# Two-layer hybrid decoder trunk on one core: fixed order at the end of the first gate/up blocks, second block's low parts last, first scale on VectorE

## Chip, cores and metric

The kernel runs on 1 core of one Trainium2 chip. The time is the device time of one execution in microseconds (us); lower is better. The kernel before took 1039.81 us, the median of 3 runs (1039.14 to 1040.87).

## What is computed

Two layers; each is a half-step SwiGLU, a mixer of sixteen attention heads (eight of one kind, eight of another), and a second half-step SwiGLU. A final RMS norm follows. Input x is 256 x 1024 float32, the inner width is 2816.

```python
def rms_norm(x, g):
    xf = x.astype(jnp.float32)
    y = xf * lax.rsqrt(jnp.mean(xf * xf, axis=-1, keepdims=True) + EPS)
    return (y * g.astype(jnp.float32)).astype(x.dtype)

def swiglu(x, w_gate, w_up, w_down):
    return (jax.nn.silu(x @ w_gate) * (x @ w_up)) @ w_down
...
    for l in range(DEPTH):
        x = x + 0.5 * swiglu(rms_norm(x, norm_ffn1[l]), w_ffn1_gate[l], w_ffn1_up[l], w_ffn1_down[l])
        x = x + hybrid_mixer(rms_norm(x, norm_mix[l]), w_in[l], ...)
        x = x + 0.5 * swiglu(rms_norm(x, norm_ffn2[l]), w_ffn2_gate[l], w_ffn2_up[l], w_ffn2_down[l])
    return rms_norm(x, norm_final)
```

## The kernel before

**Weights as a stream.** All weights are cut into 326 blocks of 128 x 1024 float32 (512 KB; a few are smaller), in order of use. `Stream.loads` (L223) issues their DMAs on SyncE into 5 raw buffers (`wraw`). `Stream.split` (L241) makes two tiles of each: ScalarE casts the block to a high part (`whi`, L254), VectorE subtracts it from the raw block for the low part (`wlo`, L283), which frees the raw buffer. There are 7 slots for such pairs of parts; a slot comes free when TensorE has read its block for the last time. A product of full precision is then high times high, high times low and low times high.

**A SwiGLU phase** (`ffn`, L593). The 2816 inner columns are 22 column blocks j of 128. For each j there is a gate block and an up block of weights. `wide` (L555) multiplies one of them: for each of 8 row blocks k one matmul of the high part with 512 columns (x high and x low side by side, L560), and one of the low part with 256 columns (x high, L562). Even j write two PSUM banks with the tag psB, odd j write psC and psD. `read` (L622) takes the banks out: ScalarE copies one half (L626), VectorE adds the other (L627), into a tile `hs`; the banks are free for the next j of the same parity after that. `finish` (L629) multiplies with the row scale on GpSimd (L635, tile `rbc`), takes Silu on ScalarE, multiplies again on GpSimd (L637, `rbc5`) and on VectorE (L639), and splits the result into `hp` high (ScalarE, L640) and low (VectorE, L642). `down` (L653) multiplies that with the down block of weights (L539 to L541) into four psA banks.

**The start.** In the first phase the products of j = 0 are made by `first_pair` (L564) and those of j = 1 by `wide`. The sums of squares of x are made meanwhile (`x_start_squares`, L437, ScalarE and GpSimd). `norm_start` (L500) adds them over partitions with two matmuls (L505), VectorE copies the two columns to `ss` (L507), and `inv_rms` (L472) takes the inverse root by a start value and two steps, 13 small operations on 128 x 2 elements on GpSimd. On VectorE the same function needs 10 operations and leaves out the factor `INV`. `norm_bcast` (L510) spreads the result with two transposing matmuls (L514), after which ScalarE writes `rbc` (L517) and `rbc5` (L521).

**Later phases.** In the other three SwiGLU phases `gu_two` (L614) works on j = 0 and j = 1 together through `two_halves` (L580): the first half of k for all four blocks, while the second half of x is still being transposed, and then the second half.

**What sets the order.** The program is recorded in the order of the Python code, and a scheduler then orders each engine's instructions by its own estimate of when each can start, with the recorded order as priority; at that point it also gives out the slots. `tc.issue_after(i)` holds an instruction behind i. Within one engine the order is then fixed, and an instruction that waits holds up those behind it.

Of the kernel before, what the change touches and what calls it, by code (L numbers as in the profile page):

```python
# [26 lines left out]
OP = mybir.AluOpType  # L27
AX = mybir.AxisListType

D, S, L, DH = 1024, 256, 2, 64  # L30
FF = 2816
KT = D // 128
# [49 lines left out]
def all_units(phases):  # L82
    return [u for ph, l in phases for u in phase_units(ph, l)]
# [227 lines left out]
def trunk(ctx, tc, xin, wst, w1st, gains, glast, cst, small, out, phases=PHASES, n_raw=5, n_hl=7):  # L311
    nc = tc.nc
    V, A, G, T = nc.vector, nc.scalar, nc.gpsimd, nc.tensor
# [7 lines left out]
    st = Stream(nc, wst, all_units(phases), rawp, hlp, n_raw, n_hl)  # L321
# [8 lines left out]
    def bank(tag):  # L330
        return ps.tile([128, 512], F32, name="ps" + tag, tag="ps" + tag, bufs=BUFS[tag])
# [40 lines left out]
    state = {}  # L372
# [97 lines left out]
    INV = -3.0 / 16  # L470

    def inv_rms(ss, eng):  # L472


        n = ss.shape[-1]
        v = base.tile([128, 2, 2], F32, name="nv", bufs=2)[:, :, :n]
        y = base.tile([128, 2], F32, name="ny", bufs=2)[:, :n]
        t = base.tile([128, 2], F32, name="nt", bufs=2)[:, :n]
        u = base.tile([128, 2], F32, name="nu", bufs=2)[:, :n]

        def plus_times(o, a, c, b, scale):
            if eng is V:
                V.scalar_tensor_tensor(o, a, c, b, op0=OP.add, op1=OP.mult)
            else:
                G.tensor_scalar(u, a, c, scale, op0=OP.add, op1=OP.mult)
                G.tensor_mul(o, u, b)

        eng.tensor_scalar(v[:, 0], ss, 1.0 / D, EPS, op0=OP.mult, op1=OP.add)
        eng.tensor_scalar(y.bitcast(I32), v[:, 0].bitcast(I32), -0.5, float(0x5F3759DF), op0=OP.mult, op1=OP.add)
        eng.tensor_scalar(v[:, 1], v[:, 0], 9.0 / 64, None, op0=OP.mult)  # L490
        eng.tensor_mul(t, y, y)
        eng.tensor_mul(t, t, v[:, 0])
        plus_times(t, t, -10.0 / 3, t, 1.0)
        plus_times(y, t, 5.0, y, 1.0)
        eng.tensor_mul(t, y, y)
        eng.tensor_mul(t, t, v[:, 1])
        plus_times(y, t, -3.0, y, INV)
        return y

    def norm_start():  # L500

        b = bank("A")
        sq = state["sq"]
        for blk in range(2):
            T.matmul(b[:, blk:blk + 1], sq[:, 0, blk * 128:(blk + 1) * 128], ones, start=True, stop=True)  # L505
        ss = base.tile([128, 2], F32, name="ss")
        V.tensor_copy(ss, b[:, :2])  # L507
        state["rs"] = inv_rms(ss, G)

    def norm_bcast(half):  # L510

# [19 lines left out]
    def three(o, hi, lo, xh, xl, first, last):  # L531
        T.matmul(o, hi, xh, start=first, stop=False, skip_group_check=True)  # L532
        T.matmul(o, hi, xl, start=False, stop=False, skip_group_check=True)  # L533
        T.matmul(o, lo, xh, start=False, stop=last, skip_group_check=True)  # L534

    def across(o, t, parts, hi, lo, first, last):

# [5 lines left out]
    def blk128(t, k):  # L543
        return t[:, k * 128:(k + 1) * 128]

    def narrow_pair(o, us, ks):

        xh, xl = state["xh"], state["xl"]
        for k in ks:
            for i, u in enumerate(us):  # L550
                hi, lo = u[1]
                three(o[:, i * S:(i + 1) * S], blk128(hi, k), blk128(lo, k), xh[:, k], xl[:, k], k == i == 0,
                      k == KT - 1)

    def wide(o, u, ks):  # L555

        hi, lo = u[1]
        for k in ks:
            x = state["x2"][:, k]
            T.matmul(o, blk128(hi, k), x.rearrange("p a t -> p (a t)"), start=k == 0, stop=k == KT - 1,  # L560
                     skip_group_check=True)
            T.matmul(o[:, S:], blk128(lo, k), x[:, 0], start=False, stop=k == KT - 1, skip_group_check=True)  # L562

    def first_pair(os, us):  # L564

# [14 lines left out]
    def two_halves(work):  # L580


        for n, (f, us) in enumerate(work):
            f(range(KT // 2))
            if n == 0:
                state.pop("late")()
        for f, us in work:
            f(range(KT // 2, KT))
            for u in us:
                st.done(u[0])  # L590


    def ffn(pi, name, l):  # L593
# [5 lines left out]
        def gu_open(j):  # L599
            b = pend[j] = [bank(t) for t in gu_tags[j % 2]]  # L600
            return b, [st.use(what, name, l, j) for what in ("gate", "up")]

        def gu(j, mid=None):
            b, us = gu_open(j)
            if j == 0 and pi == 0:
                first_pair(b, us)
                return
            for o, u in zip(b, us):
                wide(o, u, range(KT))
                st.done(u[0])  # L610
                if mid:
                    mid = mid()
# [38 lines left out]
        last = nxt == len(phases)  # L651
# [95 lines left out]
    def mixer(pi, l):  # L747
# [4 lines left out]
        def feature_one(o, u, first):  # L752
            hi, lo = u[1]
            for k in range(KT):
                three(o, blk128(hi, k), blk128(lo, k), xh[:, k], xl[:, k], first and k == 0, k == KT - 1)
            st.done(u[0])
# [577 lines left out]
```

## Time and profile before

| what | value |
|---|---|
| median of 3 runs | 1039.81 us |
| the profiled execution | 1037.38 us |
| its span, first to last instruction | 1035.6 us |
| TensorE busy | 1000.6 us (97% of the span) |
| VectorE busy | 688.5 us (66%) |
| ScalarE busy | 593.3 us (57%) |
| GpSimd busy | 326.1 us (31%) |
| chain that ended last, TensorE's share | 83% |
| mean granted TensorE clock | 0.999 |

The profiled execution is one run; it took 2.43 us less than the median of the three timed runs. In a row of the timeline the first number is the start in us from the beginning of the span, the second the us until the end of the row's last instruction; what stands in brackets is how long the engine was idle before the row and what ended that. Matmuls are pipelined: the next one starts before the row's end, so that distances are read from start to start. The trace writes x for the tile `x2`, and leaves numbers of tiles out.

### The profile page before, as it was taken

How to read it: one execution, taken by the hardware profiler on the slowest of the kernel's cores; microseconds unless marked ns; L12 is line 12 of the kernel's file. 1: busy time of each engine (PE TensorE's matmuls, PEld its weight loads, DVE VectorE, ACT ScalarE, POOL GpSimd, SP SyncE). 2: the span in 40 equal slices, each digit the busy share in tenths (PEclk: the TensorE clock that was granted, in tenths of full speed). 3: DMA queues.
4: the chain of work that ended last, by engine and by line, in shares of the span. 5: the costliest groups of instructions: out<-in, count | busy, mean ns of one | idle time of the engine just before them, and what ended most of it. 6: DMA issues, size and time to landing. Idle time of an engine off the chain costs nothing.

```text
span 1035.6 us, 16186 instructions
## 1 busy us (share of the span) xinstructions
PE 1000.6 (97%) x5861; PEld 861.0 (83%) x5861; DVE 688.5 (66%) x1187; ACT 593.3 (57%) x1137; POOL 326.1 (31%) x425
## 2 busy tenths in 40 slices
PE   9999999998998999999999999999999989999997
PEld 7788888898776888888888888889888778888885
DVE  6766666589865766566676666566986648666664
ACT  6745555457766655555565555545677747555552
POOL 3622232145641422222232223121475313222230
PEclk9999999999999999999999999999999999999999
DMA  8685776455444466666556677764543426666531
GB/s 268 241 279 186 274 240 218 145 171 157 114 126 125 154 198 196 188 197 186 163 182 203 186 234 239 262 196 138 181 131 108 143 82 208 194 209 193 193 122 41
DMA packets 52848, 188.21 MB, mean 182 GB/s; under 512 B 6368, under 2 KB 6496, under 8 KB 51616
## 3 DMA queue, kind: packets, MB, share of 16 engines
q1 hardware_dynamic: 49680, 182.04, 55.4%
q10 hardware_dynamic: 3088, 5.14, 2.0%
q8 instruction: 46, 0.75, 0.3%
q14 instruction: 34, 0.28, 0.1%
HBM read 182.04 MB, written 1.05 MB: 177 GB/s over the span
## 4 chain that ended last, share of the span: by engine, by line
PE 83%; DVE 7%; ACT 5%; issue 2%; DMA 2%; POOL 1%; ACTq 0%; POOLq 0%; DVEq 0%
PE psB L560 15%; PE psA L539 9%; PE psA L540 9%; PE psA L541 9%; PE psB L562 8%; PE psD L560 8%; PE psC L560 7%; PE psD L562 4%; PE psC L562 4%; DVE wlo L283 3%; PE psA L533 2%; PE psA L532 2%; PE psA L534 2%; ACT whi L254 1%; PE psA L398 1%
## 5 line engine op out<-in xcount | busy, mean ns | idle before, releaser
L283 DVE TENSOR_TENSOR wlo<-wraw,whi 128x1024 fp32r<-128x1024 f32 x325 | 408.2, 1259 | 242.1 <-ACT whi L254 240.5
L254 ACT CAST whi<-wraw 128x1024 fp32r<-128x1024 f32 (+1 forms) x326 | 339.5, 1044 | 304.2 <-issue 175.4
L560 PE MATMUL psB<-x,whi 128*128 128x512 f32 x688 | 243.1, 394 | 3.4 <-DVE hs L627 3.3
L635 POOL TENSOR_TENSOR hs<-hs,rbc 128x256 f32<-128x256 f32 x88 | 75.0, 853 | 380.3 <-DVE hs L627 364.6
L562 PE MATMUL psB<-x,wlo 128*128 128x256 f32 x688 | 192.5, 280 | 0.0
L560 PEld LDWEIGHTS psB<-x,whi 128*128 128x128 f32 x688 | 129.2, 188 | 32.5 <-DVE hs L627 4.3
L541 PE MATMUL psA<-wlo,hp 128*128 128x512 f32 x352 | 136.9, 389 | 0.0
L540 PE MATMUL psA<-whi,hp 128*128 128x512 f32 x352 | 136.8, 389 | 0.0
L539 PE MATMUL psA<-whi,hp 128*128 128x512 f32 x352 | 136.2, 390 | 0.0
L562 PEld LDWEIGHTS psB<-x,wlo 128*128 128x128 f32 x688 | 129.4, 188 | 1.4
L637 POOL TENSOR_TENSOR hs<-hs,rbc 128x256 f32<-128x256 f32 x88 | 102.9, 1170 | 80.5 <-ACT hs L636 80.5
L560 PE MATMUL psC<-x,whi 128*128 128x512 f32 x352 | 124.9, 392 | 0.0
L560 PE MATMUL psD<-x,whi 128*128 128x512 f32 x352 | 124.8, 392 | 0.0
L562 PE MATMUL psC<-x,wlo 128*128 128x256 f32 x352 | 98.6, 280 | 0.9 <-DVE wlo L283 0.9
L562 PE MATMUL psD<-x,wlo 128*128 128x256 f32 x352 | 98.4, 280 | 0.0
L560 PEld LDWEIGHTS psC<-x,whi 128*128 128x128 f32 x352 | 66.1, 188 | 14.5
L560 PEld LDWEIGHTS psD<-x,whi 128*128 128x128 f32 x352 | 66.1, 188 | 14.4
L541 PEld LDWEIGHTS psA<-wlo,hp 128*128 128x128 f32 x352 | 66.1, 188 | 13.9
L539 PEld LDWEIGHTS psA<-whi,hp 128*128 128x128 f32 x352 | 66.0, 188 | 13.7
L540 PEld LDWEIGHTS psA<-whi,hp 128*128 128x128 f32 x352 | 66.1, 188 | 12.3
L532 PE MATMUL psA<-x,whi 128*128 128x256 f32 x256 | 72.8, 284 | 1.2 <-ACT PT L1010 0.8
L533 PE MATMUL psA<-x,whi 128*128 128x256 f32 x256 | 72.3, 283 | 0.7 <-DVE x L380 0.7
(229 smaller groups left out, 1586.3 us busy)
## 6 DMA issues: line engine op xcount, KB each, us to landing
wraw<-in_w SPq DMA_DIRECT2D x318, 512.0 KB, 4.3
W1a<-in_w SPq DMA_DIRECT2D x4, 1024.0 KB, 6.3
W1mixn<-in_w SPq DMA_DIRECT2D x2, 1024.0 KB, 7.6
W1late<-in_w SPq DMA_DIRECT2D x2, 1024.0 KB, 6.5
KM<-KM ACTq DMA_DIRECT2D x8, 256.0 KB, 3.2
wraw<-in_w SPq DMA_DIRECT2D x4, 420.0 KB, 3.7
wraw<-in_w SPq DMA_DIRECT2D x4, 256.0 KB, 5.1
X<-in_small SPq DMA_DIRECT2D x1, 1024.0 KB, 9.5
```

The lines of the kernel that those rows point to most:

```text
L254: self.last_hi = self.nc.scalar.copy(hi[:, a:b], raw[:, a:b]).ins
L283: eng.tensor_sub(lo[:, :c], raw[:, :c], hi[:, :c].bitcast(F32))
L532: T.matmul(o, hi, xh, start=first, stop=False, skip_group_check=True)
L533: T.matmul(o, hi, xl, start=False, stop=False, skip_group_check=True)
L534: T.matmul(o, lo, xh, start=False, stop=last, skip_group_check=True)
L539: T.matmul(o, parts[:, 0, c], hi, start=first, stop=False, skip_group_check=True)
L540: T.matmul(o, parts[:, 1, c], hi, start=False, stop=False, skip_group_check=True)
L541: T.matmul(o, parts[:, 0, c], lo, start=False, stop=last, skip_group_check=True)
L560: T.matmul(o, blk128(hi, k), x.rearrange("p a t -> p (a t)"), start=k == 0, stop=k == KT - 1, skip_group_check=True)
L562: T.matmul(o[:, S:], blk128(lo, k), x[:, 0], start=False, stop=k == KT - 1, skip_group_check=True)
L635: G.tensor_mul(g, g, state["rbc"])
L637: G.tensor_mul(g, g, state["rbc5"])
```

## The change

Three edits.

- `two_halves`: the second half of k was recorded block after block. Now k = 4 comes for all entries, then k = 5 to 7 for one entry after the other, and each piece is held behind the last matmul of the piece before. For the SwiGLU phases an entry is one block; for the mixer it is a pair.
- The two blocks of j = 1 in the first phase are now multiplied by a new function `wide_apart`: all 8 matmuls of the high part, then all 8 of the low part.
- The first scale is computed by `inv_rms` on VectorE, and one more operation multiplies it with `INV`.

```diff
@@ norm_start
-        state["rs"] = inv_rms(ss, G)
+        state["rs"] = rs = inv_rms(ss, V)
+        V.tensor_scalar(rs, rs, INV, None, op0=OP.mult)
@@ three, narrow_pair, wide: each now returns its last matmul
...
+    def wide_apart(o, u):
+
+        hi, lo = u[1]
+        for k in range(KT):
+            T.matmul(o, blk128(hi, k), state["x2"][:, k].rearrange("p a t -> p (a t)"), start=k == 0, stop=k == KT - 1,
+                     skip_group_check=True)
+        for k in range(KT):
+            T.matmul(o[:, S:], blk128(lo, k), state["x2"][:, k, 0], start=False, stop=k == KT - 1,
+                     skip_group_check=True)
@@ two_halves
-        for f, us in work:
-            f(range(KT // 2, KT))
-            for u in us:
-                st.done(u[0])
+
+        last = None
+        for ks in (range(KT // 2, KT // 2 + 1), range(KT // 2 + 1, KT)):
+            for f, us in work:
+                with tc.issue_after(last) if last else nullcontext():
+                    last = f(ks)
+                if ks[-1] == KT - 1:
+                    for u in us:
+                        st.done(u[0])
@@ gu
             for o, u in zip(b, us):
-                wide(o, u, range(KT))
+                if j == 1 and pi == 0:
+                    wide_apart(o, u)
+                else:
+                    wide(o, u, range(KT))
                 st.done(u[0])
```

The buffers of the two programs lie at the same addresses, and the matmuls are as many, of the same sizes. What moves on the engines stands below at three places (L lines are those of the program shown; names with a number tell tiles apart). Outside of these places the order differs only within the first SwiGLU phase, and there up to the up block of j = 6; on SyncE nothing moves.

**Place 1: TensorE, the blocks of j = 1 in the first phase.** `whi` and `wlo` are the high and low part of a block, psC takes the gate block, psD the up block. Before:

```order
L560 MATMUL psC<-x_141,whi 128x512
L560 MATMUL psD<-x_141,whi 128x512
L562 MATMUL psC<-x_141,wlo 128x256
L560 MATMUL psC<-x_141,whi 128x512
L562 MATMUL psC<-x_141,wlo 128x256
```

Now:

```order
L590 MATMUL psB<-x_141,wlo 128x256 x4
L572 MATMUL psC<-x_141,whi 128x512 x8
L572 MATMUL psD<-x_141,whi 128x512 x8
L575 MATMUL psC<-x_141,wlo 128x256 x8
L575 MATMUL psD<-x_141,wlo 128x256 x8
L562 MATMUL psB<-x_141,whi 128x512
```

The low parts have moved behind the high parts of both blocks.

**Place 2: the first scale, on VectorE and TensorE.** On VectorE before, with only the copy of the sums (`ss`) between low parts and reads of banks:

```order
L283 TENSOR_TENSOR wlo<-wraw,whi 128x1024
L507 COPY ss<-psA 128x2
L283 TENSOR_TENSOR wlo<-wraw,whi 128x1024
L627 TENSOR_TENSOR hs<-hs,psD 128x256
L283 TENSOR_TENSOR wlo<-wraw,whi 128x1024 x2
L627 TENSOR_TENSOR hs<-hs,psB 128x256
```

VectorE now, the second part of the inverse root (four of its operations and four low parts stand between `ss` and the first row here):

```order
L649 TENSOR_TENSOR hs<-hs,psB 128x256
L492 TENSOR_TENSOR nt<-nt,nv 128x2
L283 TENSOR_TENSOR wlo<-wraw,whi 128x1024
L483 SCALAR_TENSOR_TENSOR nt<-nt 128x2
L283 TENSOR_TENSOR wlo<-wraw,whi 128x1024
L483 SCALAR_TENSOR_TENSOR ny<-nt,ny 128x2
L649 TENSOR_TENSOR hs<-hs,psC 128x256
L495 TENSOR_TENSOR nt<-ny 128x2
L496 TENSOR_TENSOR nt<-nt,nv 128x2
L483 SCALAR_TENSOR_TENSOR ny<-nt,ny 128x2
L509 TENSOR_SCALAR ny<-ny 128x2
L283 TENSOR_TENSOR wlo<-wraw,whi 128x1024
```

TensorE before, where the scale `ny` is spread (L514), ahead of the last matmul of the gate block of j = 3:

```order
L562 MATMUL psC_439<-x2_141,wlo_196 128x256
L560 MATMUL psC_439<-x2_141,whi_195 128x512
L514 MATMUL psA_372<-const_76,ny_300 128x128 x2
L562 MATMUL psC_439<-x2_141,wlo_196 128x256
L560 MATMUL psD_440<-x2_141,whi_270 128x512
```

TensorE now, inside the up block of j = 4 (psB_530), 9 of its matmuls ahead of it:

```order
L564 MATMUL psB_530<-x2_141,wlo_406 128x256
L562 MATMUL psB_530<-x2_141,whi_405 128x512
L515 MATMUL psA_370<-const_76,ny_300 128x128 x2
L564 MATMUL psB_530<-x2_141,wlo_406 128x256
L562 MATMUL psB_530<-x2_141,whi_405 128x512
```

The root has moved from GpSimd into VectorE's queue, spread among six low parts, and the spreading matmuls stand 1 + 16 + 16 + 9 = 42 matmuls further back on TensorE. The matmuls of down block 0 have moved behind the blocks of j = 5 and all but one matmul of the gate block of j = 6.

**Place 3: TensorE, the end of `two_halves` in the second SwiGLU phase** (the same rows stand in the third and fourth). psB_3611 and psB_3612 are gate and up of j = 0, psC_3613 and psD_3614 those of j = 1. Before, from the spreading matmuls on:

```order
L560 MATMUL psC_3613<-x2_3580,whi_3518 128x512
L562 MATMUL psC_3613<-x2_3580,wlo_3519 128x256
L560 MATMUL psD_3614<-x2_3580,whi_3568 128x512
L560 MATMUL psB_3611<-x2_3580,whi_3441 128x512
L562 MATMUL psB_3611<-x2_3580,wlo_3442 128x256
L560 MATMUL psB_3612<-x2_3580,whi_3483 128x512
L562 MATMUL psB_3612<-x2_3580,wlo_3484 128x256
```

Now, where the gate block of j = 0 is psB_3609:

```order
L515 MATMUL psA_3756<-const_76,ny_3644 128x128 x2
L562 MATMUL psB_3609<-x2_3578,whi_3439 128x512
L564 MATMUL psB_3609<-x2_3578,wlo_3440 128x256
L562 MATMUL psB_3609<-x2_3578,whi_3439 128x512
L564 MATMUL psB_3609<-x2_3578,wlo_3440 128x256
L562 MATMUL psB_3609<-x2_3578,whi_3439 128x512
L564 MATMUL psB_3609<-x2_3578,wlo_3440 128x256
L562 MATMUL psB_3610<-x2_3578,whi_3481 128x512
L564 MATMUL psB_3610<-x2_3578,wlo_3482 128x256
```

The gate block of j = 0 now ends with the third pair of matmuls behind the spreading matmuls. Before, two pairs each of gate 0, up 0 and gate 1 and one matmul of up 1 stood between these and its last pair.

## Rows read from the trace of the kernel before

**Rows 1.** Waits of TensorE, whole span: who waited for whom, us, times, longest.

```profile
PE psB L560 <- DVE hs L627: 3.3, 3, 1.1
...
PE psA L514 <- POOL ny L486: 2.2, 1, 2.2
...
PE psC L562 <- DVE wlo L283: 0.9, 1, 0.9
```

**Rows 2.** Timeline of TensorE, blocks of j = 1 in the first phase.

```profile
15.41 0.39 PE L560 MATMUL psD<-x,whi 128*128 128x512 f32 x1
...
16.68 0.38 PE L562 MATMUL psC<-x,wlo 128*128 128x256 f32 x1 [0.88 <-DVE wlo L283]
```

**Rows 3.** Timeline of VectorE, the low parts around there.

```profile
14.29 4.56 DVE L283 TENSOR_TENSOR wlo<-wraw,whi 128x1024 fp32r<-128x1024 f32 x2 [1.29 <-ACT whi L254]
...
19.11 1.44 DVE L283 TENSOR_TENSOR wlo<-wraw,whi 128x1024 fp32r<-128x1024 f32 x1
```

**Rows 4.** Timeline of TensorE's weight loads and matmuls, end of `first_pair`.

```profile
14.59 0.54 PEld L576 LDWEIGHTS psB<-x,wlo 128*128 128x128 f32 x4
14.71 0.63 PE L576 MATMUL psB<-x,wlo 128*128 128x256 f32 x4
```

**Rows 5.** Timeline of TensorE, the spreading matmuls of the first scale.

```profile
30.32 0.39 PE L560 MATMUL psC<-x,whi 128*128 128x512 f32 x1
32.96 0.71 PE L514 MATMUL psA<-const,ny 128*128 128x128 f32 x4 [2.25 <-POOL ny L486]
```

**Rows 6.** Timeline of GpSimd, two operations of the inverse root.

```profile
31.22 1.13 POOL L496 TENSOR_TENSOR nt<-nt,nv 128x2 f32<-128x2 f32 x1
...
32.71 0.19 POOL L486 TENSOR_TENSOR ny<-nu,ny 128x2 f32<-128x2 f32 x1
```

**Rows 7.** Timeline of VectorE, the copied sums and a later low part.

```profile
24.54 0.15 DVE L507 COPY ss<-psA 128x2 f32<-128x2 f32 x1
...
31.07 1.23 DVE L283 TENSOR_TENSOR wlo<-wraw,whi 128x1024 fp32r<-128x1024 f32 x1 [0.26 <-ACT whi L254]
```

**Rows 8.** Timeline of VectorE, its inverse root at the kernel's end: first and last of ten.

```profile
1029.67 0.15 DVE L488 TENSOR_SCALAR nv<-sq 128x1 f32<-128x1 f32 x1
...
1031.21 0.16 DVE L483 SCALAR_TENSOR_TENSOR ny<-nt,ny 128x1 f32<-128x1 f32 x1
```

**Rows 9.** Busy time by window: length, PE, PEld, DVE, ACT, POOL (count), clock, DMA, GB/s.

```profile
24.00:34.00 10.00, 7.75 (x47) 6.65 (x46) 7.74 (x11) 6.06 (x9) 7.22 (x13) 1.00 0.98 352
```

**Rows 10.** Timeline, from the spread scale to down block 0.

```profile
34.16 2.94 POOL L635 TENSOR_TENSOR hs<-hs,rbc 128x256 f32<-128x256 f32 x3 [1.25 <-ACT rbc L517]
...
38.81 0.41 ACT L640 CAST hp<-hs 128x256 fp32r<-128x256 f32 x1 [0.44 <-DVE hs L639]
...
40.71 0.63 DVE L642 TENSOR_TENSOR hp<-hs,hp 128x256 fp32r<-128x256 f32 x1
...
41.96 1.07 PE L539 MATMUL psA<-whi,hp 128*128 128x512 f32 x4
```

**Rows 11.** Timeline of TensorE, end of `two_halves` in the second SwiGLU phase.

```profile
344.63 0.40 PE L560 MATMUL psB<-x,whi 128*128 128x512 f32 x1
...
346.38 0.28 PE L562 MATMUL psD<-x,wlo 128*128 128x256 f32 x1
347.76 0.50 PE L560 MATMUL psB<-x,whi 128*128 128x512 f32 x1 [1.11 <-DVE hs L627]
```

**Rows 12.** Timeline of ScalarE and VectorE at the same place.

```profile
345.07 1.05 ACT L254 CAST whi<-wraw 128x1024 fp32r<-128x1024 f32 x1 [1.89 <-PE psB L560]
...
346.15 1.23 DVE L283 TENSOR_TENSOR wlo<-wraw,whi 128x1024 fp32r<-128x1024 f32 x1 [4.77 <-ACT whi L254]
347.29 0.42 DVE L627 TENSOR_TENSOR hs<-hs,psB 128x256 f32<-128x256 f32 x1
```

**Rows 13.** Timeline of TensorE, the same wait in the third and fourth SwiGLU phase.

```profile
533.84 0.50 PE L560 MATMUL psB<-x,whi 128*128 128x512 f32 x1 [1.10 <-DVE hs L627]
...
856.81 0.50 PE L560 MATMUL psB<-x,whi 128*128 128x512 f32 x1 [1.10 <-DVE hs L627]
```

More of the change, by code (lines that the diff above doesn't have):

```diff
@@ L533, in three @@
         T.matmul(o, hi, xl, start=False, stop=False, skip_group_check=True)
-        T.matmul(o, lo, xh, start=False, stop=last, skip_group_check=True)
+        return T.matmul(o, lo, xh, start=False, stop=last, skip_group_check=True).ins
     def across(o, t, parts, hi, lo, first, last):
@@ L551, in narrow_pair @@
                 hi, lo = u[1]
-                three(o[:, i * S:(i + 1) * S], blk128(hi, k), blk128(lo, k), xh[:, k], xl[:, k], k == i == 0,
-                      k == KT - 1)
+                last = three(o[:, i * S:(i + 1) * S], blk128(hi, k), blk128(lo, k), xh[:, k], xl[:, k], k == i == 0,
+                             k == KT - 1)
+        return last
     def wide(o, u, ks):
@@ L561, in wide @@
                      skip_group_check=True)
-            T.matmul(o[:, S:], blk128(lo, k), x[:, 0], start=False, stop=k == KT - 1, skip_group_check=True)
+            last = T.matmul(o[:, S:], blk128(lo, k), x[:, 0], start=False, stop=k == KT - 1,
+                            skip_group_check=True).ins
+        return last
+    def wide_apart(o, u):
[6 more added lines that the diff above has]
+                     skip_group_check=True)
     def first_pair(os, us):
```

## The prediction

> **What bounds the kernel now.** TensorE does. The profile's page has it busy nearly all the span, so the first view I read is the list of TensorE's waits: what it doesn't wait for can't be won back on it. Three entries belong to instructions that the diff touches [rows 1]: three waits for VectorE's read of a bank, 1.1 us each; one wait of 2.2 us for the scale from GpSimd; one of 0.9 us for a low part of weights. Together 6.4 us. The second view is the timeline at each of them, since distances from start to start give the true loss. For these I need TensorE's step: a matmul of 512 columns follows the one before after (1.07 - 0.39) / 3 = 0.227 us (last of [rows 10]), one of 256 columns after (0.63 - 0.28) / 3 = 0.117 us [rows 4]. A pair of both is 0.344 us, a block of eight pairs 2.75 us.
>
> **Edit 1, low parts last (j = 1, first phase).** The second high matmul starts at 15.41, so the next could start at 15.64; it starts at 16.68, because it needs a low part that VectorE has not made [rows 2]. Lost: 1.04 us. In the new order 16 high matmuls run from 15.2 for 16 x 0.227 = 3.6 us, to about 18.8, and then the 16 low ones until 20.7. The two low parts end at about 16.6 and 18.85, the end of their row [rows 3]; the second is first read at 18.8 + 8 x 0.117 = 19.8, so nothing waits. Next in line is the low part of gate 2, made by 20.55 [rows 3] and read at about 21.0: hidden, with 0.4 us to spare. Gain 1.04 us; the bounds are 0.6 (if that next part comes 0.4 later than now) and 1.1.
>
> The low matmuls now stand in a run of sixteen, each with its own weight load. At the end of `first_pair` such a run of four exists: four loads take 0.54 us in all, so one lasts 0.54 - 3 x 0.117 = 0.19 us, and yet the matmuls start 0.117 us apart [rows 4]; the loads overlap, and the run costs what I took. The Trainium skill, page "TensorE: Matmul & The Clock Gate", section "The mechanism", says that weight loads overlap with matmuls in flight only when the row group differs. All these loads are of the whole array, 128*128, so by that rule the run would go slower; this trace disagrees with it, and what the rule would make of the time stands among the rivals.
>
> **Edit 2, the first scale on VectorE.** The spreading matmuls could start at 30.32 + 0.23 = 30.55 and start at 32.96 [rows 5]: 2.41 us lost. GpSimd's chain ends then, at 32.9, 8.3 us behind the copied sums at 24.54 [rows 7]. It is slow because some of its operations take 1.13 instead of 0.19 us [rows 6], and the slow one at 31.22 ends within 0.1 us of the end of VectorE's low part that began at 31.07 [rows 7].
> In the new program the spreading matmuls stand 42 matmuls further back: one low one, two blocks, and 9 of a third (4 x 0.344 + 0.227 = 1.60), which is 0.12 + 5.50 + 1.60 = 7.2 us. TensorE is there at 30.55 - 1.04 + 7.2 = 36.7.
> Is the scale ready? On VectorE an operation of the root follows the one before after (1031.21 - 1029.67) / 9 = 0.17 us [rows 8], so 11 cost about 1.9 us. They stand among six low parts. The fifth of these began at 31.07 [rows 7]; add it and the sixth (2 x 1.14, a row's length less its overlap), at most 1.9 us of root, and one read of a bank (0.33): 35.6. If the gaps in which VectorE now waits for casts absorb the early operations, 34.5. Both are ahead of 36.7, so the wait is gone: gain 2.41 us. The sixth low part needs the slot of gate 3, which TensorE now leaves by 29.7 instead of holding it behind the spreading matmuls.
> Who waits for the moved spreading? `rbc`, then `finish` of j = 0, then down block 0. Now its high part is made 38.81 + 0.41 - 32.96 = 6.3 us behind the spreading, its low part 40.71 + 0.63 - 32.96 = 8.4 us behind, and down block 0 starts 9.0 us behind [rows 10]. In the new order GpSimd does five products L635 ahead of the first L637 instead of three; at 2.94 / 3 = 0.98 us each [rows 10] that makes 8.3 and 10.4 us. Down block 0 now stands behind 0.4 us of spreading, 7 matmuls (1.1), and three blocks less one matmul (8.1): 9.6 us, and its use of the low part another 8 matmuls (1.6) later, 11.2 us. It fits by 1.3 and 0.8 us. I cost it at nothing, hidden behind the blocks of j = 5 and 6; if one cast of a weight block (1.05 us, [rows 12]) falls into this chain, it costs up to 0.3 us, and with two, 1.3. Bounds for edit 2: 1.1 to 2.5 us.
>
> **Edit 3, fixed order at the end of `two_halves`.** In the second SwiGLU phase TensorE is through at 346.38 + 0.12 = 346.50 and starts the gate block of j = 2 at 347.76 [rows 11]: 1.26 us. The chain: the last high matmul of gate 0, at 344.63, frees a slot; ScalarE's cast starts at 345.07, VectorE's low part at 346.15, and only behind that, in VectorE's order, comes the read of the bank at 347.29 [rows 11, 12]. In the new order gate 0 ends with the third pair behind the spreading matmuls. Between them and its last pair stood six pairs and one high matmul; now two pairs: 4 x 0.344 + 0.227 = 1.60 us earlier. ScalarE and VectorE keep their order, and their waits (1.89 and 4.77 us, [rows 12]) show that nothing else holds them. The bank is then free at 347.76 - 1.60 = 346.16, ahead of 346.50. What is late next: the bank of up 0, read one low part and one read later (1.14 + 0.33), due one block (2.75) later; that fits. Gain 1.26 us, three times [rows 13]; bounds 0.8 (had TensorE to wait 0.4 in spite of this) and 1.26 each. In the mixer the order stays as it is.
>
> **Small terms.** The first matmul behind a wait lasts 0.1 us more (0.50 against 0.40 in [rows 11]); five waits less save 0.5 us. The 11 operations added to VectorE and the 13 taken from GpSimd have no other cost: the low parts of j = 4 and 5, which they delay by 2 us at most, are made 2 to 7 us ahead of their use.
>
> **Sum.** 1.04 + 2.41 + 3 x 1.26 + 0.5 = 7.7 us. The phases behind each place run with TensorE at full load or follow it at a fixed distance, so nothing absorbs it. Against the profiled execution that is 1037.38 - 7.7 = 1029.7. The median of the timed runs is 2.43 us above that execution; against it, 1039.81 - 7.7 = **1032.1 us**.
>
> **The rivals.** About 0.2% (2 us) is what a measurement of this kernel can tell from no change.
>
> - *Only part arrives.* Margins of 0.3 to 0.8 us at places 2 and 3 are taken from another order's distances. If the three bank waits stay by half and down block 0 waits 1.3 us, the gain is 7.7 - 1.9 - 1.3 = 4.5: 1035.3 us. For it: the margins are thinner than what one cast takes. Against: nothing new stands ahead of these reads. Chance 0.17, still faster.
> - *VectorE becomes the bound, and the kernel slower.* VectorE was busy 7.74 of 10 us from 24 to 34 [rows 9], and the root adds to it. If its operations there, each between two low parts, cost as much as GpSimd's slow ones (1.13 us, [rows 6]) instead of 0.17, the scale is ready 11 x 0.96 = 10.6 us later, at 45 to 46; TensorE waits from 36.7 on, loses 9 us, and the whole comes to 1039.8 - 7.7 + 9 = 1041.1. It decides for slower from the point where the scale is later than 36.7 + 7.7 = 44.4. Against it: at the end VectorE's root runs at 0.17 us with a large operation in between as well, and VectorE still has idle gaps here. The Trainium skill, page "Perfetto Trace Analysis", section "Optimizing Scalar/DVE Operations", warns of a cost per instruction and advises to move work off a saturated VectorE, even to GpSimd, which is the opposite of this edit; by that rule the time is the one of this rival, and the trace supports only the load, not the price. Chance 0.05.
> - *Low parts in a row are slow.* If loads are not hidden there, 16 x 0.19 = 3.0 us come back in place 1: 1035.1. [Rows 4] speak against it. This is what the rule on weight loads, cited above from the Trainium skill, would make of it. Chance 0.02.
> - *Nothing changes.* The stream of weights could set the pace: DMA was busy 98% from 24 to 34 [rows 9]. Then the gains of the first phase would go (3.5 + 0.2 us), and with the later ones eaten by the next refill all would: 1039 to 1040. Against: a block lands every 1.5 us there (352 GB/s for 0.52 MB), TensorE needs one every 2.75. Chance 0.04.
>
> **How the numbers follow.** The forecast has 0.72: 1030 to 1033.5, the bounds of the edits (0.6 + 1.1 + 2.4 = 4.1 to 8) and the 1.7 us by which the three runs differed. Eight in ten need the partial case's better half too: 1029.5 to 1035.8. Faster by over 0.2%: 0.72 + 0.17 + 0.02 = 0.91; within 0.2%: 0.04; slower: 0.05.
>
> **What would show it.** In TensorE's waits the three entries of [rows 1] are gone. The low matmuls of j = 1 follow the high ones without a gap and gate 2 starts near 20.8. The spreading matmuls start near 36.7 with no wait, the scale on VectorE being ready at 34.5 to 35.6. Down block 0 starts near 46.3 with no wait. In each later phase the block of j = 2 follows the last low matmul after 0.12 us. A TensorE wait for `hp` or for the scale would show the first two rivals; the same waits under other names, the last.

## The result, and the profile after

The changed kernel takes **1032.56 us** (median of 6 runs, 1030.33 to 1034.86), the kernel before, on the same chip, 1040.68 us (6 runs, 1039.14 to 1041.76). The ratio is 0.9924, with a 95% interval of 0.9908 to 0.9940: 7.9 us faster, 6.2 to 9.6. A second set of runs, told below, gave 0.9921 (0.9905 to 0.9937). The forecast was 1032.1 us, 7.7 faster. The profiled execution of after has 1032.01 us and a span of 1030.2.

The first part of the page shows what moved between engines: 11 operations to VectorE, 13 away from GpSimd.

```profile
PE 1001.7 (97%) x5861; PEld 864.2 (84%) x5861; DVE 691.9 (67%) x1198; ACT 593.8 (58%) x1137; POOL 319.6 (31%) x412
```

The list of TensorE's waits in after begins so (who waited for whom: us in total, times, longest):

```profile
PE psA L540 <- ACT late L1134: 3.5, 2, 1.8
PE psB L1053 <- ACT whi L254: 3.3, 1, 3.3
PE psD L1070 <- ACT PcT L991: 2.0, 2, 1.0
PE psB L1053 <- DVE qs L801: 2.0, 1, 2.0
```

The three entries of [rows 1] are gone. The entries that are left belong to the mixers; the second and the fourth, at the first scores, were 2.8 us together in this profile of before, and are 5.3 here. Whether the change makes them grow is taken up below.

Now the places, in order. First the blocks of j = 1, on TensorE's timeline and on VectorE's; in this execution TensorE is 0.40 us later than in the one of before already ahead of these blocks, where it waits for the input's parts, so that 0.40 is to be taken from the times:

```profile
15.58 2.03 PE L572 MATMUL psC<-x,whi 128*128 128x512 f32 x8
17.44 2.03 PE L572 MATMUL psD<-x,whi 128*128 128x512 f32 x8
19.32 1.11 PE L575 MATMUL psC<-x,wlo 128*128 128x256 f32 x8
20.27 1.11 PE L575 MATMUL psD<-x,wlo 128*128 128x256 f32 x8
21.21 0.39 PE L562 MATMUL psB<-x,whi 128*128 128x512 f32 x1
```
```profile
14.70 4.55 DVE L283 TENSOR_TENSOR wlo<-wraw,whi 128x1024 fp32r<-128x1024 f32 x2 [1.29 <-ACT whi L254]
...
19.51 1.43 DVE L283 TENSOR_TENSOR wlo<-wraw,whi 128x1024 fp32r<-128x1024 f32 x1
```

No row of TensorE has a wait in brackets. The two low parts are ready at 19.25 (the end of the row of two) and read from 19.32 and 20.27 on; the next is ready at 20.94, ahead of 21.21. Gate 2 starts at 21.21 - 0.40 = 20.81, where 20.8 was forecast.

Then the first scale: the root between VectorE's low parts, and the spreading matmuls.

```profile
25.25 0.15 DVE L507 COPY ss<-psA 128x2 f32<-128x2 f32 x1
...
26.45 0.16 DVE L488 TENSOR_SCALAR nv<-ss 128x2 f32<-128x2 f32 x1
...
34.27 0.17 DVE L509 TENSOR_SCALAR ny<-ny 128x2 f32<-128x2 f32 x1
```
```profile
36.94 0.40 PE L562 MATMUL psB<-x,whi 128*128 128x512 f32 x1
37.17 0.61 PE L515 MATMUL psA<-const,ny 128*128 128x128 f32 x4
```

The scale is there at 34.44, TensorE comes to it at 37.17 and does not wait, where it waited 2.25 us in [rows 5]. An operation of the root costs 0.15 to 0.17 us, also between two low parts.

Behind it, the chain to down block 0, on GpSimd, ScalarE, VectorE and TensorE:

```profile
38.26 4.50 POOL L657 TENSOR_TENSOR hs<-hs,rbc 128x256 f32<-128x256 f32 x5 [18.41 <-DVE hs L649]
...
44.47 0.41 ACT L662 CAST hp<-hs 128x256 fp32r<-128x256 f32 x1 [0.38 <-DVE hs L661]
...
46.92 0.96 DVE L664 TENSOR_TENSOR hp<-hs,hp 128x256 fp32r<-128x256 f32 x1
...
46.99 1.07 PE L540 MATMUL psA<-whi,hp 128*128 128x512 f32 x4
...
48.60 0.39 PE L541 MATMUL psA<-whi,hp 128*128 128x512 f32 x1
```

Down block 0 has no wait. The high part is made at 44.88, 2.1 us early; the low one at 47.88 and is read at 48.60, so 0.72 us were left.

Last, the end of `two_halves` in the second SwiGLU phase, on VectorE and on TensorE:

```profile
344.05 0.42 DVE L649 TENSOR_TENSOR hs<-hs,psB 128x256 f32<-128x256 f32 x1
...
344.74 0.28 PE L564 MATMUL psD<-x,wlo 128*128 128x256 f32 x1
344.86 0.39 PE L562 MATMUL psB<-x,whi 128*128 128x512 f32 x1
```

The bank is read by 344.47; the block of j = 2 follows the last low matmul after 0.12 us, where [rows 11] have 347.76 - 346.38 = 1.38.

To add up, the same matmul is looked for in both traces, and the time between two of them compared. TensorE does 5861 matmuls in both kernels. From number 91 to number 326 (the first phase behind its opening) before takes 46.44 us, after 42.64: 3.80 less. From 1801 to 2101 (over the first of the three ends) it is 55.63 against 54.29, from 2101 to 3101 (the second) 188.15 against 186.78, from 4701 to 5001 (the third) 56.09 against 54.69: 4.11 less. Together 7.91 us; the forecast had 7.7. This adds up the three places alone; the two profiled executions differ by 5.4 us as a whole (spans of 1035.6 and 1030.2), and where the rest went is taken up below too.

### The profile page after: what moved, and what is told of

Same layout as the page of the kernel before. It is cut to its first block, busy times and chain, and to the rows that moved or that the text cites. A ratio compares the mean times of both kernels' runs of the same rounds, so it can differ in the third digit from the quotient of the medians.

```text
span 1030.2 us, 16186 instructions
## 1 busy us (share of the span) xinstructions
PE 1001.7 (97%) x5861; PEld 864.2 (84%) x5861; DVE 691.9 (67%) x1198; ACT 593.8 (58%) x1137; POOL 319.6 (31%) x412
## 3 DMA queue, kind: packets, MB, share of 16 engines
HBM read 182.04 MB, written 1.05 MB: 178 GB/s over the span
## 4 chain that ended last, share of the span: by engine, by line
PE 88%; ACT 4%; DVE 4%; issue 1%; DMA 1%; POOL 1%; ACTq 0%; POOLq 0%; DVEq 0%
PE psB L562 15%; PE psA L540 9%; PE psA L541 9%; PE psA L542 9%; PE psB L564 8%; PE psC L562 8%; PE psD L562 8%; PE psC L564 4%; PE psD L564 4%; PE psA L534 2%; PE psA L533 2%; PE psA L535 2%; DVE wlo L283 1%; PE psD L1039 1%; ACT whi L254 1%
## 5 line engine op out<-in xcount | busy, mean ns | idle before, releaser
L562 PE MATMUL psC<-x,whi 128*128 128x512 f32 x344 | 121.8, 392 | 0.0
L562 PE MATMUL psD<-x,whi 128*128 128x512 f32 x344 | 121.7, 392 | 0.0
L564 PE MATMUL psC<-x,wlo 128*128 128x256 f32 x344 | 96.4, 280 | 0.0
```

The source lines that it names most:

```text
L564: last = T.matmul(o[:, S:], blk128(lo, k), x[:, 0], start=False, stop=k == KT - 1, skip_group_check=True).ins
```

## The experiments

Four questions: is each edit worth what its wait was, is it the engine or the place of the spreading matmuls that counts, what became of the lead in the mixers, and can more be had there. All ratios are against runs of the kernel before on the same chip. TensorE's clock has two levels here, 2.4 GHz (a granted clock of 1.00 in the rows) and 1.2 GHz (0.50).

**Each edit by itself.** Four kernels, each made from the changed one by taking edits back:

`order_only`, the scale and the order of j = 1 as before:

```diff
-        state["rs"] = rs = inv_rms(ss, V)
-        V.tensor_scalar(rs, rs, INV, None, op0=OP.mult)
+        state["rs"] = inv_rms(ss, G)
-                if j == 1 and pi == 0:
-                    wide_apart(o, u)
-                else:
-                    wide(o, u, range(KT))
+                wide(o, u, range(KT))
```

`start_only`, `two_halves` as before:

```diff
-        for ks in (range(KT // 2, KT // 2 + 1), range(KT // 2 + 1, KT)):
...
+        for f, us in work:
+            f(range(KT // 2, KT))
```

`scale_only` takes back `two_halves` and the order of j = 1 with the same lines, `lows_only` takes back `two_halves` and the scale.

> Edit 3 alone (fixed order at the three ends of the SwiGLU half steps; the first phase as before). Theory, each edit is worth the TensorE waits that it removes: 3 x 1.26 and 0.3 of restarts, 4.1 us, ratio 0.9961 (0.9951 to 0.9969); in the profile down block 0 still starts near 42, the block of j = 2 follows the last low matmul after 0.12 us at each site. Rival, what is won is partly given back at the next refill of weights or in the mixer: 2 us, ratio 0.998. Rival, the edits only work together: no change, 0.9990 to 1.0010.

Measured: 0.9964 (0.9951 to 0.9977; 1037.16 us), 3.7 us faster. Over the three ends the trace has 54.23, 186.76 and 54.69 us, as in the full change; the wait for the scale is still there (1.9 us). The theory holds.

> Edits 1 and 2 alone (first phase as in the changed kernel, the ends of the half steps as before). Theory, the gains add: 1.04 + 2.41 + 0.2 of restarts = 3.65 us, ratio 0.9965 (0.9955 to 0.9975); the three bank waits of 1.1 us are still in the list. Rival, the lead of the first phase is lost by the mixer (the profile of the changed kernel shows its lead shrink from 3.1 to 1.1 us at the mixer's first block of slopes): 1.5 us or less, ratio 0.9985 or more.

Measured: 0.9947 (0.9932 to 0.9962; 1036.01 us), 5.5 us faster. The first phase takes 42.64 us, as in the full change, and the three waits of 1.1 us are still listed. The rival is out, but the gain is more than the waits.

> Edit 2 alone (the first scale on VectorE, j = 1 in its old order, the ends of the half steps as before). Theory: 2.41 + 0.1 of restart = 2.5 us, ratio 0.9976 (0.9966 to 0.9989); the spreading matmuls start unwaited near 37.5, j = 1 still waits 1.04 us for its low part. Rival, VectorE's root delays the low parts that follow: no change or slower, ratio 0.9995 or more, with new TensorE waits for low parts between 30 and 40.

Measured: 0.9952 (0.9937 to 0.9967; 1035.92 us), 5.0 us faster, and the interval leaves the 2.5 us of the theory out. The spreading matmuls start at 38.38 without a wait. So the wait is gone as reckoned, and something else is gained with it. What was expected of j = 1 did not come: in this profile, and in that of order_only, TensorE runs at half clock from 10.8 on, comes some 2 us later to the blocks of j = 1, and does not wait for their low part although the old order stands there. In such executions edit 1 has nothing to win.

> Edit 1 alone (low parts of j = 1 last; the scale on GpSimd as before, and its spreading matmuls only five places further back; the ends of the half steps as before). Theory, the two places are not independent: TensorE comes 1.04 us earlier to a scale that GpSimd has at 32.9 as before, so that the wait there grows by what was won: spreading near 32.9, gain 0 to 0.5 us, ratio 0.9995 to 1.0000. Rival, the terms add for each edit by itself: 1.1 us, ratio 0.9989, the spreading matmuls then starting near 31.9.

Measured: 1.0006 (0.9994 to 1.0017; 1042.04 us): nothing gained. The low parts no longer hold TensorE, but the list has a longer wait for the scale:

```profile
PE psA L514 <- POOL ny L486: 3.6, 1, 3.6
```

In this execution GpSimd has the scale only at 34.67: it began with the sums at 25.75, and six of its 13 operations took the long 1.1 to 1.2 us, where five did in before's. So TensorE came 1.04 us earlier to a scale that was not earlier (1.8 us later in this execution), as the theory has it, and the rival's 1.1 us lie outside the interval: edit 1 is worth something only when the scale is no longer late.

**What a wait costs beside itself.** The profile of lows_only shows TensorE at half clock right behind its wait, and so does that of order_only; before's first profile does not. Its granted clock over the whole span was 0.999, though, while 21 timed runs of before had 0.991 to 0.996. Hence two runs: before once more, for a profile, and before with the wait filled, so that TensorE waits as long but is busy (`fill_scale`, in `norm_bcast`, ahead of the spreading matmuls; a manual order holds them behind the eighth high matmul of the gate of j = 3; besides, a few instructions of the first phase behind them change places):

```diff
+        state["fill"] = [T.matmul(b[:, :256], zero[:, :128], zero, start=True, stop=True).ins
+                         for _ in range(16 if half and "filled" not in state else 0)]
```

> The kernel before with the wait for the first scale left in place, but filled: 16 products of zeros (256 columns each, into the bank that the spreading matmuls then overwrite) stand ahead of them, about 16 x 0.117 = 1.9 of the 2.2 us that TensorE waits there. Edit 2 alone gained 5.0 us by its ratio where 2.5 were reckoned. Theory, the idle costs more than itself: in most executions TensorE is granted 1.2 instead of 2.4 GHz for 3.4 us soon behind it (the profiles with edit 3 alone and with edit 1 alone show 3.41 us at 34.7 and 6.83 us at 33.5), half of which is lost; filled, the stretch is gone and the kernel gains 1 to 1.7 us, ratio 0.9984 to 0.9990, no half clock between 30 and 42 us, the spreading matmuls still at about 33. Rival, the rest of edit 2's gain comes from VectorE and GpSimd themselves: ratio 1.0000, the half-clock stretch near 34 as in the other two.

> The kernel before once more, for a second profile. Theory, the wait for the first scale is followed by a half-clock stretch in most executions (in the profiles with edit 3 alone and with edit 1 alone it is, in the first profile of before it is not, and the granted clock of before's runs is 0.991 to 0.997 where that profile has 0.999): a stretch of 3.4 us that begins between 31 and 38, span 1037 to 1041. Rival, such stretches come from the mixers alone: none there.

The second profile of before, TensorE's timeline and the windows around it (length, busy times, granted clock, DMA):

```profile
33.04 0.71 PE L514 MATMUL psA<-const,ny 128*128 128x128 f32 x4 [2.22 <-POOL ny L486]
...
34.92 0.63 PE L560 MATMUL psD<-x,whi 128*128 128x512 f32 x1
35.35 0.41 PE L562 MATMUL psD<-x,wlo 128*128 128x256 f32 x1
...
37.72 0.39 PE L560 MATMUL psD<-x,whi 128*128 128x512 f32 x1
```
```profile
33.85:37.20 3.35, 3.35 (x12) 2.84 (x11) 1.56 (x2) 2.98 (x6) 2.96 (x4) 0.50 0.82 232
```

The theory holds. The clock falls to 0.50 at 33.8, 0.7 us behind the end of the wait, for 3.41 us; a pair of matmuls takes 0.64 us (34.92 to 35.56) instead of 0.35, and 12 matmuls fit where before's first profile has 21. From the 177th matmul, with which the wait ends, to the 201st, before_again takes 5.61 us, before 4.03: 1.58 us more. The same kernel, the same wait, and another time.

In the filled kernel:

```profile
30.60 1.92 PE L513 MATMUL psA<-zero 128*128 128x256 bf16 x16
32.98 0.71 PE L516 MATMUL psA<-const,ny 128*128 128x128 f32 x4 [0.46 <-POOL ny L486]
```
```profile
33.20:42.00 8.80, 8.80 (x53) 7.80 (x53) 5.71 (x7) 6.61 (x13) 7.77 (x8) 1.00 0.58 198
```

The spreading matmuls stand where they stood, no real work is done earlier, the clock stays at 1.00, and the kernel is faster: 0.9979 (0.9967 to 0.9991; 1038.10 us), 2.2 us (0.9 to 3.4). From number 91 to 326, the zeros left out, its profile takes 46.41 us, the first profile of before 46.44 and the second 48.01: the filled kernel is no faster there than an execution that keeps its clock. So the wait of 2.4 us costs more than itself: of the four profiles that have it unfilled (before, before_again, order_only, lows_only) three have half clock between 33 and 41, of the nine others none.

This can account for a part of the 2.5 us that edit 2 gained beyond its wait; how large a part is not shown. The 21 runs of before have a mean granted clock of 0.9931, scale_only's six 0.9960, and a straight line through the 21 gives 5.7 us for 0.01 of clock, so 1.7 us for the difference. The line is a rough one: on the two other chips the runs of before give 8.8 and 4.6 us, and fill_scale's clock (0.9955 against 0.9945) makes 0.9 us of its 2.2 by the first of these.

**Engine or place.** The root goes back to GpSimd, and the spreading matmuls are held at the place that they have after the change (`gp_late`, and the same kernel again, `gp_late2`):

```diff
-        state["rs"] = rs = inv_rms(ss, V)
-        V.tensor_scalar(rs, rs, INV, None, op0=OP.mult)
+        state["rs"] = inv_rms(ss, G)
...
+                    if j == 4 and pi == 0 and u is us[1]:
+                        for m in state["spread"]:
+                            tc.add_manual_dep(m, state["ninth"].name, mybir.DependencyInfo(
```

> The changed kernel with the first scale back on GpSimd, and the spreading matmuls held at the place that they have in the changed kernel (behind the ninth matmul of the third block after the gate of j = 3). Theory, the place decides, not the engine: GpSimd has the scale near 33, as before, and TensorE comes to it at 36.7, so that nothing waits: the time of the changed kernel, ratio 0.9924 (0.991 to 0.994). Rival, the engine decides: GpSimd's root is as late as 36.7 or its products behind the scale come late and down block 0 waits, 1 to 2.5 us lost: ratio 0.9935 to 0.995 and a wait of TensorE at the spreading matmuls or at the first down block.

> The kernel with the root on GpSimd and the spreading matmuls at the later place, once more. Its first profile follows the changed kernel within 0.45 us through the whole first phase, and yet its median was 4 us longer; the profile put the loss in the mixers (half-clock stretches at 235.8, 297.2 and 751.2 us, against 11.2 alone in the second profile of the changed kernel). Theory, the difference lies in where half-clock stretches fall and moves between sets of runs: ratio nearer to the changed kernel's now, 0.992 to 0.995, and the stretches in other places. Rival, something steady in the mixers is slower with the root on GpSimd: ratio 0.996 again, and the same waits as in its first profile.

Measured: 0.9963 (0.9949 to 0.9977; 1036.49 us), and again 0.9962 (0.9948 to 0.9975; 1036.15 us). For the first phase the theory holds: 42.64 and 42.66 us from number 91 to 326, as in the changed kernel; GpSimd has the scale at 32.2 (35.1 in gp_late2), and the spreading matmuls start unwaited:

```profile
36.77 0.61 PE L515 MATMUL psA<-const,ny 128*128 128x128 f32 x4
```

So there the place alone brings the gain; VectorE was not needed for it. Yet the whole is 4 us slower than the changed kernel, twice, so the theory that this is chance falls. It is lost in the mixers, whose instructions stand in the same order on every engine. In the first mixer the two kernels part at VectorE's `nm`, a small operation: gp_late, and then the changed kernel (its second profile):

```profile
275.84 1.28 POOL L797 TENSOR_TENSOR rotmq<-rotmq,SW 128x512 f32<-128x512 f32 x1
276.19 0.95 DVE L1014 TENSOR_SCALAR nm<-mx 128x4 f32<-128x4 f32 x1
277.24 0.51 ACT L1016 ACTIVATE P<-P,nm 128x256 f32<-128x256 f32 x1 [2.07 <-DVE sm L1026]
```
```profile
276.41 0.40 POOL L1023 TENSOR_TENSOR P<-P,sm 128x128 f32<-128x128 f32 x1
276.55 0.28 DVE L1008 TENSOR_SCALAR nm<-mx 128x4 f32<-128x4 f32 x1
276.92 0.51 ACT L1010 ACTIVATE P<-P,nm 128x256 f32<-128x256 f32 x1 [0.82 <-DVE sm L1020]
```

In both, `nm` begins while GpSimd works and ends 0.02 us behind GpSimd's operation. VectorE comes 0.6 us later here in gp_late (it idled 0.30 us 3 us before, for which the trace names no cause, and a low part behind that took 1.68 us instead of 1.45), so `nm` falls into the next operation of GpSimd, which is long. It takes 0.95 us instead of 0.28 (0.96 in gp_late2), and ScalarE, which needs what follows it, is 1.27 us later from there on, counted from matmul 1596. Some 12 us on, ScalarE, VectorE and GpSimd are 1.84 us later; TensorE gets a wait of 0.98 (0.79 in gp_late2) and then one of 2.34 us (1.85 in the changed kernel), and half clock from 297 on:

```profile
296.91 0.51 PE L540 MATMUL psA<-whi,mixn 128*128 128x512 f32 x1 [2.34 <-ACT late L1140]
```
```profile
297.30:300.60 3.30, 3.30 (x10) 2.54 (x9) 3.25 (x12) 2.35 (x6) 0.81 (x1) 0.50 0.74 250
```

From number 1596 to 1801 (this stretch of the mixer) gp_late takes 37.85 us, gp_late2 37.62, the changed kernel 34.45 and 34.50; from 3101 to 4701 (up to and into the second mixer) it is 265.6 and 266.1 against 264.1 twice. GpSimd's root is not the cause by itself: the five profiles of before, before_again, order_only, lows_only and fill_scale have it too, and take 34.3 to 34.6 from 1596 to 1801. What differs is when things start, and so which operations of VectorE and GpSimd meet; why they start so in these two runs was not settled.

**The lead in the mixers.** In the first profile of after TensorE idles 3.34 us at the first scores of the first mixer, and runs at half clock from 236.8 on.

> The changed kernel once more, for a second profile and on the same chip as the next. Its first profile loses 2 us of its lead at the mixer's first scores (the copies of the keys land 6.5 to 7.1 us after their issue instead of 5.3, TensorE idles 3.3 us and then runs 3.4 us at half clock). Theory, that is this one execution's: ratio 0.9924 again, the copies landing in 5 to 6 us, and the half-clock stretches in other places or absent. Rival, the change causes it (weights and copies now meet): landing above 6.4 us and half clock at about 237 and 742 again.

Measured: 0.9921 (0.9905 to 0.9937; 1032.25 us), no half clock in the mixers in this profile (one stretch at 11.2, in the opening), and the first mixer's copies of the keys land after 5.1 to 5.3 us. The theory holds. It is true that the first scores start at 235.45 us here and at 235.48 in the first profile, though the first of the copies was issued at 230.0 here and at 228.2 there. But this is a coincidence of two landing times, as other profiles show: from issue to landing, before_again, without the change, and fill_mixer, told next, have

```profile
DMA to landing us min/median/max: 6.6/7.0/7.4
```
```profile
DMA to landing us min/median/max: 5.0/5.3/5.7
```

In fill_mixer the first copy is issued at 228.2 as in the first profile of after, and lands at 233.8, 1.5 us sooner. In before the two copies take 5.3 us each. In the twelve profiles other than split_keys' the first scores of the first mixer start 0.1 us behind the first copy's landing. So the wait there grows and shrinks by what the copies take in an execution, with the change and without it (3.5 us of wait in before_again); the rival is out.

`fill_mixer`, in `nsa_s`, ahead of the scores:

```diff
+            if h == 0:
+                with tc.issue_after(state["feat"]):
+                    for _ in range(14):
+                        T.matmul(s1[:, :256], zero[:, :128], zero, start=True, stop=True)
```

> The changed kernel with 14 products of zeros (about 1.6 us, into the bank that the scores then overwrite) behind the first feature block of each mixer, where TensorE waits 1.5 to 3.3 us for the copies of the keys. The planner also moves a few later operations of the mixer. Theory, half-clock stretches follow such idle times and cost 1.7 us each: 1 to 3 us less than the changed kernel, ratio 0.9895 to 0.9915. Rival, the mixer is held by VectorE (11.7 of 12 us busy ahead of the scores), which takes back whatever TensorE gains: the ratio of the changed kernel, 0.992, within 0.001.

Measured: 0.9954 (0.9938 to 0.9969; 1035.27 us), 3 us slower than the changed kernel; both theories miss. In the first mixer the wait at the first scores is filled and no half clock follows it, but the planner, which reckons the added products as work, writes the rest of the mixer in another order, and this one has longer waits:

```profile
264.81 0.52 PE L1030 MATMUL psA<-const,P 128*128 128x128 f32 x3 [1.58 <-DVE rotmq L787]
267.71 1.22 PE L1074 MATMUL psD<-PcT,late 128*128 128x256 f32 x2 [2.38 <-ACT PcT L991]
```

The experiment is confounded by that, and says nothing on what the clock costs there.

`split_keys`, in `stack_k` and `repeat_k` (which is also called one step later):

```diff
                 A.copy(KK[g][half[g], 0], src)
+                A.dma_start(KK[g][half[1 - g], 0].bitcast(F32), KK[g][half[g], 0].bitcast(F32))
...
-                A.dma_start(KK[g][half[1 - g]].bitcast(F32), KK[g][half[g]].bitcast(F32))
+                A.dma_start(KK[g][half[1 - g], 1].bitcast(F32), KK[g][half[g], 1].bitcast(F32))
```

> The changed kernel, in which the copies of the keys to the other half of the partitions are sent in two parts, the high parts as soon as ScalarE has cast them, the low parts when VectorE has made them: four copies of 128 KB for two of 256 KB. Theory, the bytes of one copy set when it lands: half of them left after the low parts are made land 1 to 2.5 us earlier, TensorE's wait at the first scores (1.4 to 3.3 us in the profiles of the changed kernel) shrinks by as much in each of the two mixers, and with it the half-clock stretch behind it: ratio 0.988 to 0.991. Rival, the copies stand behind weights that are in flight (landing at 235.2 to 235.3 us in both profiles of the changed kernel, whether issued at 228.2 or 230.0): they land when they do now, and the two additional issues on ScalarE cost nothing or 0.5 us: ratio 0.992 to 0.993.

Measured: 0.9931 (0.9916 to 0.9946; 1032.69 us), no gain. TensorE starts the scores at 233.93, 1.5 us earlier than in either profile of after, with the high parts, and then waits for the low ones:

```profile
233.93 0.40 PE L1054 MATMUL psB<-KK,qs 128*128 128x512 f32 x1
236.26 0.47 PE L1054 MATMUL psB<-KK,qs 128*128 128x512 f32 x1 [1.93 <-DMA KK<-KK]
```

Half the bytes, issued at 230.0 as in the second profile of after, land no earlier: a copy of 128 KB takes 5.0 to 6.2 us. So the bytes do not set the landing, and the theory falls. The rival's time comes; its reason, weights in flight, was not tested. No version was found that beats the change.

## Why the prediction was right, step by step

- *Edit 1, 1.04 us.* Gate 2 starts 1.07 us earlier (20.81 with the 0.40 taken off, 21.88 in before). Alone it gains nothing (lows_only); the sum could use the term because edit 2 stands behind it. Sixteen low matmuls follow at (1.11 - 0.28) / 7 = 0.119 us. The rule of the Trainium skill's page "TensorE: Matmul & The Clock Gate", section "The mechanism", that weight loads overlap only when the row group differs, would make it 0.19; the trace disagrees, now over sixteen in a row. The Trainium skill's same section also lets a load go ahead that aims at the array's background weight buffer; no row here shows where a load goes, so the page as a whole is not refuted. In executions with half clock in the opening the term is nothing, since the wait is not there (order_only, scale_only).
- *Edit 2, 2.41 us.* Edits 1 and 2 together were reckoned as 3.45 and 0.2 of restarts, and the trace has 3.80. The scale was forecast at 34.5 to 35.6 and is there at 34.44, or 34.04 with the 0.40 taken off, half a microsecond ahead of the range, because the fifth low part begins at 30.55 (the 0.40 taken off) and not at 31.07 as in before; the spreading matmuls at 36.7, and start at 36.77. The rival "VectorE becomes the bound" is refuted by its own price: 0.15 to 0.17 us for an operation, not 1.13. (The Trainium skill's page "Perfetto Trace Analysis", section "Optimizing Scalar/DVE Operations", which the prediction cites there, is milder than the prediction has it: it says that moving work off a saturated VectorE may make sense, and that between VectorE and GpSimd it might not help.) What the term left out is the clock: the wait also costs 1.58 us in the execution of before in which half clock follows it. The 2.43 us that the prediction adds for the median above the profiled execution may be of this kind in part: that execution keeps its full clock from 5 us to its last few, with a mean of 0.999, where the timed runs of before have 0.991 to 0.998.
- *Down block 0.* Forecast at 46.3 with 1.3 and 0.8 us to spare; it starts at 46.6 (0.40 taken off) and had 2.1 and 0.72.
- *Edit 3, 3 x 1.26 us.* 4.11 us with the restarts, 4.08 reckoned; the bank is free 0.39 us ahead, 0.34 reckoned. Alone it gains 3.7 us by the runs.
- *"So nothing absorbs it".* This step was wrong in two ways, both small. A part is given back in both profiles of after: from number 326 to 1161 they take 150.79 and 150.70 us, before's two 150.46; from 3101 to 4701 264.12 and 264.11, before's 263.77 and 263.56. That is 0.3 and 0.4 us or more. And behind each place more than the change decides: between 1161 and 1386, around the first scores, the two profiles of after take 26.83 and 24.78 us, those of before 24.89 and 26.90. That difference of 2 us is as large as an edit, but it comes with the landing of the copies and the clock of the one execution, not with the lead. The opening does the same: with half clock there TensorE takes 16.25 us from number 1 to 91 (second profile of after), without it 14.15 (the first).

So the step from waits to time was sound, and that the total came out as close as it did is in part luck: the sum left out that more is won where the wait for the scale was, and that some is given back later. By the waits alone it is 7.9 us; edits 1 and 2 alone and edit 3 alone gain 5.5 and 3.7, 9.2 together; the whole gains 7.9 to 8.2. The intervals (1.5 us to either side) hold both the sum and its shortfall, so how much of either there is on average stays open.

## What to carry to other kernels

A wait of TensorE is to be priced with what its clock does behind it: look at the granted clock of the next few microseconds, in more than one execution, before the gain of removing it is written down. If the consumer of a late result can stand further back in the order, moving it may do all that a faster engine would do in that phase: here both brought the same 42.64 us. What it does to the phases behind is to be measured too: the same kernel lost 4 us there. A wait that differs by 2 us from one execution to the next, as the one for the copies of the keys, is not to be laid to a change from one profile of each kernel.

## What the runs showed of the hardware

- Half clock came in stretches of about 3.4 us or twice that, and began behind pauses of TensorE much shorter than the stretch: 0.82 us at 7.9 in order_only (clock 0.50 from 10.8 on), 2.22 us at 30.8 in before_again. As long a pause went without it in another execution: 2.25 us at 30.7 in before.
- In gp_late's profile the granted clock stands at 0.95 for most of the first 700 us, a third value beside the two levels, and TensorE is no slower for it: 262 matmuls from 50 to 100 us, 261 in the second profile of after at 1.00.

```profile
50.00:100.00 50.00, 50.00 (x262) 42.95 (x262) 34.86 (x47) 26.61 (x43) 14.01 (x15) 0.95 0.68 239
```
```profile
50.00:100.00 50.00, 50.00 (x261) 42.89 (x260) 35.35 (x49) 27.64 (x46) 13.30 (x14) 1.00 0.68 237
```

- GpSimd and VectorE hold each other up. In the seven profiles with the root on GpSimd, 36 of its 91 operations began while VectorE was making a low part; all 36 took 1.05 to 1.27 us and ended 0.05 to 0.08 us behind that low part, as in [rows 6] and [rows 7], and the other 55 took 0.19 to 0.22. The mixers' products of 256 columns (`P`) show the same: 113 of 624 in the thirteen profiles began within a low part or within VectorE's `KM` or `qs`; all ended 0.47 or 0.48 us behind it and took 0.79 to 1.65 us, the 511 others 0.60 to 0.62. The other way, 174 of 208 operations `nm` on VectorE began within an operation of GpSimd and ended 0.02 to 0.09 us behind it, after up to 0.96 us; the 34 others took 0.15 to 0.17. So the length goes by what the operation falls into, and not by its work. The Trainium skill, page "GPSIMD Engine Reference", section "1. Specifications", says that GpSimd shares its ways into SBUF with VectorE and meets it when VectorE reads two operands from there; the low parts, `KM` and `qs` read two, and agree with it.
